# A two-layer trunk whose FFN operands are cut by token halves instead of interleaved tokens

## The chip, the cores and the metric

The program runs on one core of one Trainium2 chip. The metric is the device time of one execution in microseconds (us). Before the change the median of three runs is 2257.63 us (2257.1 to 2259.68).

## The reference

x holds 1024 tokens of 1024 features in float32. Layer 0 mixes tokens by attention, layer 1 by a gated recurrence; each layer then has a SwiGLU FFN of width 2816, and every sub-layer is wrapped in two RMS norms.

```python
def swiglu(h, w_gate, w_up, w_down):
    return (jax.nn.silu(h @ w_gate) * (h @ w_up)) @ w_down

for layer in range(2):
    h = rmsnorm(x, norm_mix_pre[layer])
    m = attention_mixer(h, ...) if layer == 0 else recurrent_mixer(h, ...)   # ends in (...) @ w_out
    x = x + rmsnorm(m, norm_mix_post[layer])
    h = rmsnorm(x, norm_ffn_pre[layer])
    x = x + rmsnorm(swiglu(h, w_gate[layer], w_up[layer], w_down[layer]), norm_ffn_post[layer])
```

## The kernel before

**Stages.** Attention with its input projection; `out_product` (the mixer's output projection, its post-norm, the residual, the FFN's pre-norm); `gate_up`; `down` (with the post-norm, the residual, and the pre-norm of what follows); `recurrent`; then `out_product`, `gate_up` and `down` of layer 1. A token tile is 128 tokens, numbered 0 to 7. A product in almost full precision is made of three passes over fp32r operands: hi times hi, hi times lo, lo times hi, where hi is a cast on ACT and lo the remainder, subtracted on DVE. Every operand therefore costs one ACT and one DVE instruction.

**out_product.** Tiles 0, 1, 2 and then 3, 4, 5 are made in triples, six PSUM buffers each, by three passes; tiles 6 and 7 follow in plain fp32. After each tile `post_norm` runs: multiply by the post gain (DVE, L212), sum of squares (ACT, L164), reciprocal root (POOL, L167 and L168), residual (DVE, L215), store; `pre_norm` then takes a second sum of squares, scales the rows on ACT (L189), transposes them on PE into two PSUM buffers (L197), and hands them to a sink.

**gate_up.** Each 256 columns of a weight times the hidden state is one Strassen product of the Winograd kind: 7 products of 128 x 512 instead of 8, of 4 blocks and 3 passes each, 84 matmuls. There are 11 pairs of columns for gate and 11 for up in a layer. The left operands (A11, A12, S2, S3, S1, S4, A22) are made from the weight tile, which ACT first scales by the FFN's norm weights (L478); the right ones are seven combinations of the hidden state's four blocks B11, B12, B21, B22: features in halves by tokens in halves. `HiddenS` holds them: its group b0 is B11 and B21, b1 is B22, b2 the four sums.

**Which tokens are a half.** Before, the two halves of the tokens are interleaved: in every tile of 128, the first 64 tokens are of one half and the last 64 of the other. So each tile fills 64 columns of all seven operands (L80 to L96), and after four tiles the first 256 of their 512 columns are complete. The first gate pair of a layer uses this: `strassen` runs for `early` (256 columns, from tiles 0 to 3) and again for `late`.

**down.** It uses the same scheme and gives its rows in the same interleaving: `norm(r, a)` holds two runs of 64 tokens, with r the half and a the block. `rows()` loads x and stores the result for each as two DMAs of 64 rows; the last stage's second halves are stored over ACT's queue. The blocks of r = 1 are normed first, while the last products run; then for a = 0 to 3 the last product's eleven steps are followed by `norm(0, a)`. After layer 0, `HiddenT` takes the rows, and a pair (r, a) lies in token half a//2, which `recurrent` reads in halves of 512 tokens, half 0 first (L757 to L764).

**What sets the order.** A scheduler with a timeline model orders the instructions of each engine when the kernel is built; each engine then runs its list in order. Buffers are rings (`bufs=`): a tile waits until the last reader of the one before it in the ring is done. `self.psum()` has six PSUM buffers, `psum_t` (transposes) two. DMAs are issued in order on SP's queue.

Of the kernel before, what the change touches and what calls it, by code (L numbers as in the profile page):

```python
# [8 lines left out]
F32 = mybir.dt.float32  # L9
# [6 lines left out]
P = 128  # L16
# [11 lines left out]
def rows(t, x):  # L28

    if not isinstance(t, tuple):  # L30
        return [(slice(0, P), x[t * P:(t + 1) * P, :])]
    r, a = t
    o = [2 * a * P + k * P + 64 * r for k in range(2)]
    return [(slice(64 * k, 64 * k + 64), x[o[k]:o[k] + 64, :]) for k in range(2)]


class HiddenT:
# [7 lines left out]
    def take(self, t, pst, scratch, pool):  # L45
        nc = self.nc
        if isinstance(t, tuple):
            r, a = t
            hh, hl = (h.rearrange("p k (a t r i) -> p k a t r i", a=2, t=2, r=2)[:, :, a % 2, :, r, :]
                      for h in self.half[a // 2])  # L50
            pst = [ps.rearrange("p a (t i) -> p a t i", t=2) for ps in pst]
        else:
            tok = slice((t % 4) * P, (t % 4) * P + P)
            hh, hl = (h[:, :, tok] for h in self.half[t // 4])
        for q, ps in enumerate(pst):
            hi = hh[:, 4 * q:4 * q + 4]
            self.last = nc.scalar.copy(hi, ps).ins
            nc.vector.tensor_tensor(hl[:, 4 * q:4 * q + 4], ps, hi.bitcast(F32), op=ALU.subtract)


class HiddenS:
# [8 lines left out]
    def __init__(self, trunk, pool):  # L70
        self.nc, self.uid = trunk.nc, trunk.uid
        self.g = [[pool.tile([P, n, 4, 512], F32R, tag=f"b{i}{z}", name=trunk.uid("hS"))
                   for z in range(2)] for i, (_, n) in enumerate(self.GROUPS)]

    def op(self, i, z, kt, cols):
        for (i0, n), g in zip(self.GROUPS, self.g):
            if i0 <= i < i0 + n:
                return g[z][:, i - i0, kt, cols]

    def take(self, t, pst, scratch, pool):  # L80
        nc = self.nc
        hf = scratch.rearrange("p (q a b) -> p q a b", q=2, a=4)
        for q, ps in enumerate(pst):
            nc.scalar.copy(hf[:, q], ps)
        lo, hi = slice(0, 64), slice(64, P)
        b11, b12, b21, b22 = hf[:, 0, :, lo], hf[:, 0, :, hi], hf[:, 1, :, lo], hf[:, 1, :, hi]
        tf = pool.tile([P, 4, 4, 64], F32, tag="tf", bufs=1, name=self.uid("tf"))
        sub = lambda o, x, y: nc.vector.tensor_tensor(o, x, y, op=ALU.subtract)  # L88
        sub(tf[:, 0], b12, b11)
        sub(tf[:, 2], b22, b12)  # L90
        sub(tf[:, 1], b22, tf[:, 0])
        sub(tf[:, 3], tf[:, 1], b21)
        cols = slice(64 * t, 64 * t + 64)
        for src, (h, l) in zip((hf[:, :, :, lo], hf[:, 1:2, :, hi], tf), self.g):
            self.last = nc.scalar.copy(h[:, :, :, cols], src).ins  # L95
            sub(l[:, :, :, cols], src, h[:, :, :, cols].bitcast(F32))  # L96


class Trunk:
# [101 lines left out]
    def post_norm(self, ms, mg, x_src, x_dst, t, gpost, sink, pool):  # L201
# [4 lines left out]
        for d, s in rows(t, x_src):  # L206
            self.load(x[d, :], s)
# [8 lines left out]
        for k, (d, s) in enumerate(rows(t, x_dst)):  # L216
            (nc.scalar if k and sink is None else nc.sync).dma_start(s, x[d, :])
        if sink is not None:
            self.pre_norm(pool, x, mg, None, sink, t, self.psum_t)
# [188 lines left out]
    def out_product(self, ap, aT, w, x_src, x_dst, gpost_v, sink, kts):  # L408
# [4 lines left out]
        def act(kt, t0, n, pool, bufs, tag="act"):  # L413
            a = pool.tile([P, 384], F32, tag=tag, bufs=bufs, name=self.uid("act"))[:, :n * P]
            nc.sync.dma_start(a, aT[kt][:, t0 * P:(t0 + n) * P])
            return a
# [8 lines left out]
        def norm(t, ps):  # L425
            mg = ap.tile([P, D], F32, tag="mg", bufs=3, name=self.uid("mg"))
            ms = [(slice(i * 512, (i + 1) * 512), p) for i, p in enumerate(ps)]
            self.post_norm(ms, mg, x_src, x_dst, t, gpost, sink, ap)

        gpost = None  # L430
        for t0 in (0, 3):
            pst = [[self.psum() for _ in range(2)] for _ in range(3)]
            for kt in kts:
                pool, bufs = (self.apool, 1) if t0 == 0 and kt == kts[0] else (ap, 3)
                a = act(kt, t0, 3, pool, bufs)
                wh, wl = self.split(wv[kt], 2, 512)
                ah, al = (pool.tile([P, 384], F32R, tag=n, bufs=bufs, name=self.uid(n)) for n in ("ah", "al"))
# [6 lines left out]
            if gpost is None:  # L444
                gpost = self.gain(ap, "gpost", gpost_v)
            for t in range(3):
                norm(t0 + t, pst[t])

        rows, acts = [], []
        for i, kt in enumerate(kts):  # L450
# [3 lines left out]
            acts.append(act(kt, 6, 2, ap, 3, ("act", "ah", "al")[i % 3]))  # L454
# [7 lines left out]
    def gate_up(self, ap, hS, wg, wu, gain, gO):  # L462
# [4 lines left out]
        nc = self.nc  # L467

        def load(w, j, tags, after=None):

            a = []
            for k in range(2):
                raw = self.main.tile([P, 4, 256], F32, tag="raw", bufs=3, name=self.uid("raw"))
                src = w[k * 512:(k + 1) * 512, j * 256:(j + 1) * 256].rearrange("(k p) c -> p k c", p=P)
                nc.sync.dma_start(raw, src)
                with self.tc.issue_after(after) if after else nullcontext():
                    for i in range(4):
                        nc.scalar.activation(raw[:, i], raw[:, i], AF.Copy, scale=gain[:, 4 * k + i:4 * k + i + 1])  # L478
                a.append(raw)
            a11, a21 = a[0][:, :, 0:P], a[0][:, :, P:256]  # L480
            a12, a22 = a[1][:, :, 0:P], a[1][:, :, P:256]
            q = {}
            for name, tag in zip(("A11", "A12", "S2", "S3", "S1", "S4", "A22"), tags):
                pool, bufs = (self.main, 8) if tag == "w" else (ap, 6)
                q[name] = pool.tile([P, 2, 4, P], F32R, tag=tag, bufs=bufs, name=self.uid("q"))

            def split(n, src):
                t = q[n]
                self.last = nc.scalar.copy(t[:, 0], src).ins  # L489
                nc.vector.tensor_tensor(t[:, 1], src, t[:, 0].bitcast(F32), op=ALU.subtract)  # L490

            tt = nc.vector.tensor_tensor
            split("A11", a11)
            split("A12", a12)
            split("A22", a22)
            tt(a22, a21, a22, op=ALU.add)
            tt(a21, a11, a21, op=ALU.subtract)
            tt(a11, a22, a11, op=ALU.subtract)  # L498
            split("S2", a11)
            split("S3", a21)  # L500
            split("S1", a22)
            tt(a12, a12, a11, op=ALU.subtract)
            split("S4", a12)
            return q

        def product(ps, a, i, cols):
            for kt in range(4):
                bh, bl = hS.op(i, 0, kt, cols), hS.op(i, 1, kt, cols)
# [5 lines left out]
        tt = nc.vector.tensor_tensor  # L514

        def blocks():
            return [ap.tile([P, 512], F32, tag="c", bufs=11, name=self.uid("c")) for _ in range(4)]

        def strassen(c, q, cols):

            s1, u2, u3, c22 = c

            def new():
                return self.psum()[:, :cols.stop - cols.start]

            nc.scalar.copy(s1, product(new(), q["A11"], 0, cols))
            p2 = product(new(), q["A12"], 1, cols)
            tt(u2, product(new(), q["S2"], 4, cols), s1, op=ALU.add)
            tt(s1, p2, s1, op=ALU.add)
            tt(u3, product(new(), q["S3"], 5, cols), u2, op=ALU.add)  # L530
            p5 = product(new(), q["S1"], 3, cols)
            tt(u2, p5, u2, op=ALU.add)
            tt(c22, p5, u3, op=ALU.add)
            tt(u2, product(new(), q["S4"], 2, cols), u2, op=ALU.add)
            tt(u3, u3, product(new(), q["A22"], 6, cols), op=ALU.subtract)

        full, early, late = slice(0, 512), slice(0, 256), slice(256, 512)
        for j in range(NF // 2):
            qg = load(wg, j, ["w"] * 7, self.last if j == 1 else None)
            if j == 0:  # L540

                first = self.main.tile([P, 4, 256], F32, tag="w", bufs=8, name=self.uid("first"))
                strassen([first[:, i] for i in range(4)], qg, early)
                cg = blocks()
                strassen([o[:, late] for o in cg], qg, late)
                for i, o in enumerate(cg):
                    nc.scalar.activation(o[:, early], first[:, i], AF.Silu)
                    nc.scalar.activation(o[:, late], o[:, late], AF.Silu)
            else:
                cg = blocks()  # L550
                strassen(cg, qg, full)
# [394 lines left out]
```

## Time and profile before

| what | value |
|---|---|
| runs | 2257.63 us median (2257.1 to 2259.68) |
| profiled execution | 2262.01 us, of which the span is 2260.2 us |
| granted TensorE clock, mean | 0.993 of full |
| out_product, layer 0 | 518.5 to 616.2 us |
| gate_up, layer 0 | 616.2 to 1047.9 us |
| down, layer 0 | 1047.9 to 1273.8 us |
| recurrent | 1273.8 to 1501.5 us |
| out_product, gate_up, down of layer 1 | from 1501.5, 1599.2 and 2029.1 us |
| last matmul, end of the span | 2250.3, 2260.2 us |

A stage here begins with the start of its first matmul. A row of the view by windows gives a stretch, its length, and then for PE, PEld (PE's weight loads), DVE, ACT and POOL the busy us with the number of instructions, then the mean granted PE clock, the DMA engines' share and their GB/s. A row of groups names line, engine, operation and tile, the count, the busy us and mean ns of one, and behind the second bar the idle us before them with what ended it. A timeline row is start us, us, engine, line, operation, and in brackets the idle time before and what ended it.

### The profile page before, as it was taken

The page shows a single profiled execution, that of the slowest core. Times are in us where ns is not written, and L with a number is a line of the kernel's source. Part 1 is how long each engine was busy: PE and PEld are TensorE (multiplying, and loading weights), DVE is VectorE, ACT ScalarE, POOL GpSimd, SP SyncE. Part 2 cuts the span into 40 slices and gives each one's busy share as a digit, 9 for nine tenths or more (in the row PEclk, how much of TensorE's full clock was granted, in tenths as well). Part 3 has the DMA queues.
Part 4 walks back from the last instruction along what each step waited for, and adds up shares of the span by engine and source line. Part 5 has one row for each costly group of instructions (what it writes and reads, how often), then busy time and mean ns, then how long its engine had stood idle before and what let it go on. Part 6 is the DMA issues. An engine that isn't in the chain of part 4 may idle for free. (4 is left out here: it accounts for less than half of the span.)

```text
span 2260.2 us, 30583 instructions
## 1 busy us (share of the span) xinstructions
PE 2201.2 (97%) x11136; PEld 1802.0 (80%) x11136; DVE 1551.9 (69%) x2514; ACT 1149.1 (51%) x2132; POOL 168.3 (7%) x370
## 2 busy tenths in 40 slices
PE   7999999999999999999999999999999999999997
PEld 6887888877678888888887777887788888888875
DVE  5676765464677767675866787536777767668665
ACT  4544455464665454532446567527755444424443
POOL 2111212131100000000001100001100000000010
PEclk9999999999999999999999999999999999999998
DMA  4101011124623333334558511358233333327466
GB/s 161 52 20 52 20 48 41 59 97 132 230 83 104 114 115 108 102 118 175 187 148 251 155 56 41 94 175 269 76 125 108 100 115 104 107 98 274 126 205 196
DMA packets 187271, 273.63 MB, mean 121 GB/s; under 512 B 13936, under 2 KB 115312, under 8 KB 187120
## 3 DMA queue, kind: packets, MB, share of 16 engines
q1 hardware_dynamic: 186480, 269.58, 38.0%
q10 hardware_dynamic: 640, 2.10, 0.3%
q8 instruction: 87, 1.43, 0.3%
q14 instruction: 64, 0.52, 0.1%
HBM read 206.09 MB, written 65.54 MB: 120 GB/s over the span
## 5 line engine op out<-in xcount | busy, mean ns | idle before, releaser
L509 PE MATMUL ps<-hS,q 128*128 128x512 f32 (+1 forms) x1288 | 490.9, 382 | 3.1 <-ACT hS L95 3.1
L510 PE MATMUL ps<-hS,q 128*128 128x512 f32 (+1 forms) x1288 | 490.9, 381 | 0.0
L511 PE MATMUL ps<-hS,q 128*128 128x512 f32 (+1 forms) x1288 | 489.9, 381 | 0.0
L490 DVE TENSOR_TENSOR q<-raw,q 128x512 fp32r<-128x512 f32 x308 | 204.7, 686 | 179.2 <-ACT q L489 178.7
L509 PEld LDWEIGHTS ps<-hS,q 128*128 128x128 f32 x1288 | 243.3, 189 | 50.2 <-ACT hS L95 3.9
L510 PEld LDWEIGHTS ps<-hS,q 128*128 128x128 f32 x1288 | 243.9, 189 | 46.7 <-DVE hS L88 0.4
L511 PEld LDWEIGHTS ps<-hS,q 128*128 128x128 f32 x1288 | 244.0, 189 | 45.8
L489 ACT CAST q<-raw 128x512 fp32r<-128x512 f32 x308 | 177.8, 616 | 168.8 <-DVE raw L498 130.4
L590 PE MATMUL ps<-o,o 128*128 128x512 f32 x616 | 240.9, 392 | 0.9 <-DVE o L585 0.8
L591 PE MATMUL ps<-o,o 128*128 128x512 f32 x616 | 238.2, 391 | 0.7 <-DVE o L701 0.7
L589 PE MATMUL ps<-o,o 128*128 128x512 f32 x616 | 221.1, 393 | 9.0 <-ACT o L700 5.5
L584 ACT CAST o<-raw 128x512 fp32r<-128x512 f32 x206 | 123.6, 620 | 193.8 <-PE ps L591 56.0
L478 ACT ACTIVATE raw<-raw,gcol 128x256 f32<-128x256 f32 x352 | 150.2, 498 | 139.0 <-DMA raw<-in_ffn_w_up_dram 71.8
L585 DVE TENSOR_TENSOR o<-raw,o 128x512 fp32r<-128x512 f32 x206 | 137.9, 688 | 66.4 <-ACT o L584 65.6
L589 PEld LDWEIGHTS ps<-o,o 128*128 128x128 f32 x616 | 115.7, 188 | 37.2 <-ACT o L700 7.7
L144 DVE TENSOR_TENSOR wlo<-raw,whi 128x1024 fp32r<-128x1024 f32 x76 | 93.4, 1230 | 66.0 <-ACT whi L143 65.1
L590 PEld LDWEIGHTS ps<-o,o 128*128 128x128 f32 x616 | 116.2, 189 | 26.6 <-DVE o L585 2.9
L591 PEld LDWEIGHTS ps<-o,o 128*128 128x128 f32 x616 | 116.1, 188 | 25.5 <-DVE o L701 1.6
L167 POOL TENSOR_SCALAR rs<-ss 128x1 f32<-128x1 f32 x64 | 31.8, 496 | 1270.2 <-ACT junk L164 1171.0
L143 ACT CAST whi<-raw 128x1024 fp32r<-128x1024 f32 x76 | 79.8, 1052 | 58.5 <-PE ps L155 24.7
L358 ACT COPY pt<-tr 128x512 f32<-128x512 f32 (+1 forms) x128 | 65.5, 527 | 78.5 <-PE tr L354 78.0
L154 PE MATMUL psq<-hT,whi 128*128 128x512 f32 x256 | 101.2, 395 | 1.1 <-DVE v L253 1.1
(185 smaller groups left out, 4237.6 us busy)
## 6 DMA issues: line engine op xcount, KB each, us to landing
raw<-in_ffn_w_down_dram SPq DMA_DIRECT2D x96, 256.0 KB, 4.6
raw<-in_ffn_w_gate_dram SPq DMA_DIRECT2D x44, 512.0 KB, 4.1
raw<-in_ffn_w_up_dram SPq DMA_DIRECT2D x44, 512.0 KB, 4.1
gS<-c SPq DMA_DIRECT2D x88, 256.0 KB, 3.6
raw<-gS SPq DMA_DIRECT2D x88, 256.0 KB, 3.0
gA<-c SPq DMA_DIRECT2D x66, 256.0 KB, 3.4
raw<-in_attn_w_in_dram SPq DMA_DIRECT2D x24, 512.0 KB, 3.9
raw<-in_attn_w_out_dram SPq DMA_DIRECT2D x24, 512.0 KB, 4.3
```

The source lines that it names most:

```text
L154: nc.tensor.matmul(ps, wh[:, kt, cols], hh[:, kt, :], start=kt == 0, stop=False)
L478: nc.scalar.activation(raw[:, i], raw[:, i], AF.Copy, scale=gain[:, 4 * k + i:4 * k + i + 1])
L489: self.last = nc.scalar.copy(t[:, 0], src).ins
L490: nc.vector.tensor_tensor(t[:, 1], src, t[:, 0].bitcast(F32), op=ALU.subtract)
L509: nc.tensor.matmul(ps, a[:, 0, kt, :], bh, start=kt == 0, stop=False)
L510: nc.tensor.matmul(ps, a[:, 0, kt, :], bl, start=False, stop=False)
L511: nc.tensor.matmul(ps, a[:, 1, kt, :], bh, start=False, stop=kt == 3)
L584: nc.scalar.copy(t[:, 0], src)
L585: tt(t[:, 1], src, t[:, 0].bitcast(F32), op=ALU.subtract)
L589: nc.tensor.matmul(ps, a[0], b[:, 0], start=first, stop=False)
L590: nc.tensor.matmul(ps, a[0], b[:, 1], start=False, stop=False)
L591: nc.tensor.matmul(ps, a[1], b[:, 0], start=False, stop=last)
```

## The change

`HiddenS` now cuts the tokens into halves: tiles 0 to 3 are the first half, 4 to 7 the second. After tiles 0 to 3 group b0 (B11 and B21) is complete in all 512 columns, while b1 and b2 get their columns from tiles 4 to 7 alone: tile t (4 or more) combines its own transposes with those of tile t-4, which are kept as `f`. `out_product` makes its tiles in the order (0, 1, 4), (2, 3, 5), 6, 7, and norms the second triple as 2, 5, 3. In `gate_up` the `early`/`late` split is gone. The two products that need only b0 (A11 times B11, A12 times B21) of four column pairs, gate 0, up 0, gate 1 and up 1, stand first; those of gate 0 and up 0 are then added up, those of gate 1 and up 1 stay in four PSUM buffers until their pairs come. For these four pairs the left half of the weights is loaded apart, ahead of the whole tile. The FFN's norm weights are no longer multiplied into the weights on ACT but into the rows on DVE (L191, with `g`, loaded once a layer into the place of the first step's operands). `mg` and `act` have two buffers instead of three. In `down` a norm's rows are 128 tokens in order, tile 4r + a, with one DMA for load and one for store; the last stage stores on SP alone.

```diff
 class HiddenT:
     def take(self, t, pst, scratch, pool):
-        if isinstance(t, tuple):
-            r, a = t
-            hh, hl = (h.rearrange("p k (a t r i) -> p k a t r i", a=2, t=2, r=2)[:, :, a % 2, :, r, :]
-                      for h in self.half[a // 2])
...
+        tok = slice((t % 4) * P, (t % 4) * P + P)
+        hh, hl = (h[:, :, tok] for h in self.half[t // 4])
 class HiddenS:
+    def take(self, t, ps, scratch, pool):
+        cols = slice((t % 4) * P, (t % 4) * P + P)
...
+        def split(h, l, src):
+            cast(h, src)
+            sub(l, src, h.bitcast(F32))
+        b0, b1, b2 = self.g
+        if t < 4:
+            f = self.f[t] = new("f", 2)
+            for q in range(2):
+                split(b0[0][:, q, :, cols], b0[1][:, q, :, cols], ps[q])
+                cast(f[:, q], ps[q])
+            return
+        b12, b22 = ps
+        f, e = self.f[t - 4], new("e", 1)
+        cast(e[:, 1], b12)
+        sub(f[:, 0], b12, f[:, 0])
+        split(b1[0][:, 0, :, cols], b1[1][:, 0, :, cols], b22)
+        sub(e[:, 1], b22, e[:, 1])
+        sub(e[:, 0], b22, f[:, 0])
+        sub(f[:, 1], f[:, 1], e[:, 0])
+        for src, i in ((e, slice(1, 3)), (f, slice(0, 4, 3))):
+            split(b2[0][:, i, :, cols], b2[1][:, i, :, cols], src)
 def post_norm
-        for d, s in rows(t, x_src):
-            self.load(x[d, :], s)
+        self.load(x, x_src[t * P:(t + 1) * P, :])
...
-            self.pre_norm(pool, x, mg, None, sink, t, self.psum_t)
+            self.pre_norm(pool, x, mg, g, sink, t, self.psum_t)
 def out_product
-            mg = ap.tile([P, D], F32, tag="mg", bufs=3, name=self.uid("mg"))
+            mg = ap.tile([P, D], F32, tag="mg", bufs=2, name=self.uid("mg"))
...
-        for t0 in (0, 3):
+        for ts in ((0, 1, 4), (2, 3, 5)):
...
+                g = self.gain(self.apool, "first", g_v)
+            for i in ((0, 1, 2) if ts[0] == 0 else (0, 2, 1)):
+                norm(ts[i], pst[i])
 def gate_up
-                        nc.scalar.activation(raw[:, i], raw[:, i], AF.Copy, scale=gain[:, 4 * k + i:4 * k + i + 1])
...
+        def begin(w, j):
+            r = raw()
+            for k in range(2):
+                nc.sync.dma_start(r[:, k], rows(w, k, j * 256, P))
+            a11, a12 = operand(r[:, 0]), operand(r[:, 1])
+            return product(a11, 0), product(a12, 1)
...
+        begun = {}
+        for i in range(4):
+            w, j = (wg, wu)[i % 2], i // 2
+            begun[i] = begin(w, j)
+            if i < 2:
+                begun[i] = sums(*begun[i])
         for j in range(NF // 2):
-            if j == 0:
-                first = self.main.tile([P, 4, 256], F32, tag="w", bufs=8, name=self.uid("first"))
-                strassen([first[:, i] for i in range(4)], qg, early)
-                cg = blocks()
-                strassen([o[:, late] for o in cg], qg, late)
...
+            cg = blocks(wg, j, begun.get(2 * j))
+            for o in cg:
+                nc.scalar.activation(o, o, AF.Silu)
+            cu = blocks(wu, j, begun.get(2 * j + 1), hS.last if j == 0 else None)
 def down
-                    self.post_norm(ms, mg, x_src, x_dst, (r, a), gpost, sink, ap)
+                    self.post_norm(ms, mg, x_src, x_dst, 4 * r + a, gpost, sink, ap)
```

The order of PE's list at the end of layer 0's `down`, before the change: `ps2071` is the last product's last block, `hT1930` and `hT1931` are hi and lo of token half 0 in `HiddenT`, and L154 and L155 are matmuls of `recurrent`.

```order
L589 MATMUL ps2071_11942<-o2019_11675,o2070_11939 128x512
L590 MATMUL ps2071_11942<-o2019_11675,o2070_11939 128x512
L591 MATMUL ps2071_11942<-o2019_11675,o2070_11939 128x512
L154 MATMUL ps2097_12056<-hT1930_11253,whi2081_12030 128x512
L154 MATMUL ps2100_12090<-hT1930_11253,whi2084_12037 128x512
L154 MATMUL ps2103_12124<-hT1930_11253,whi2087_12044 128x512
L155 MATMUL ps2097_12056<-hT1931_11254,whi2081_12030 128x512
```

The same place after the change: `ps2066` is the last product's last block, `m1722` and `m1723` are the rows of the last two norms (tiles 2 and 3), `hT1925` is hi of token half 0 and `hT1927` hi of half 1.

```order
L605 MATMUL ps2066_11648<-o2014_11387,o2065_11645 128x512
L606 MATMUL ps2066_11648<-o2014_11387,o2065_11645 128x512
L201 MATMUL pst2058_11619<-ident_63,m1722_9722 128x128 x4
L201 MATMUL pst2059_11624<-ident_63,m1722_9722 128x128 x4
L201 MATMUL pst2073_11700<-ident_63,m1723_9723 128x128 x4
L201 MATMUL pst2074_11705<-ident_63,m1723_9723 128x128 x4
L158 MATMUL ps2092_11760<-hT1925_10973,whi2076_11734 128x512
L158 MATMUL ps2095_11794<-hT1925_10973,whi2079_11741 128x512
L158 MATMUL ps2098_11828<-hT1925_10973,whi2082_11748 128x512
L158 MATMUL ps2101_11862<-hT1927_10975,whi2076_11734 128x512
```

The transposes of the last two tiles, which stood some 25 rows and more behind the first matmuls of `recurrent`, now stand ahead of them.

ACT's list where layer 0's `gate_up` begins, after the change: `pst1273` and `pst1274` are the transposes of tile 7, `hS1056` is b1, `hS1058` b2 (hi), `raw1304` and `raw1305` the whole weight tiles of the first gate pair, `q1307` the operand S2, L570 the silu.

```order
L75 COPY e1275_6507<-pst1273_6497 128x512
L75 CAST hS1056_5602<-pst1274_6502 128x4x128
L75 CAST hS1058_5604<-e1275_6507 128x8x128
L75 CAST hS1058_5604<-f1233_6356 128x2x4x128
L522 COPY c1282_6626<-ps1279_6599 128x512
L493 CAST q1306_6746<-raw1305_6744 128x512
L522 COPY c1291_6667<-ps1288_6640 128x512
L570 ACT_TABLE_LOAD
L570 ACTIVATE c1281_6625<-c1281_6625 128x512
L493 CAST q1307_6752<-raw1304_6742 128x512
```

S2's cast, the first operand needed behind the products that stand first, comes after all four pieces of tile 7 and after a table load.

PE's list there: `pst1231` and `pst1232` are tile 3's transposes, `hS1054` and `hS1055` hi and lo of b0, `q1277`, `q1278`, `q1286` and `q1287` the first two left operands of gate 0 and of up 0.

```order
L201 MATMUL pst1231_6346<-ident_63,mg1223_6324 128x128 x4
L201 MATMUL pst1232_6351<-ident_63,mg1223_6324 128x128 x4
L507 MATMUL ps1279_6599<-hS1054_5600,q1277_6593 128x512
L507 MATMUL ps1280_6612<-hS1054_5600,q1278_6596 128x512
L507 MATMUL ps1288_6640<-hS1054_5600,q1286_6634 128x512
L507 MATMUL ps1289_6653<-hS1054_5600,q1287_6637 128x512
L508 MATMUL ps1279_6599<-hS1055_5601,q1277_6593 128x512
```

All four open products of the first two pairs follow tile 3's transposes at once, 512 columns wide, where before there were 256-wide ones from `early`.

201 lines of the change are left out of this document (89 added, 112 removed).

## The prediction

> **What bounds the kernel now.** I read the busy shares first, then a table of windows by stage, then the waits of PE.
>
> ```profile
> PE 2201.2 (97%) x11136; PEld 1802.0 (80%) x11136; DVE 1551.9 (69%) x2514; ACT 1149.1 (51%) x2132; POOL 168.3 (7%) x370
> 616.20:1047.90 431.70, 426.32 (x1958) 356.36 (x1957) 316.29 (x520) 213.92 (x429) 3.51 (x7) 0.99 0.32 102
> 642.00:1047.90 405.90, 405.90 (x1816) 337.12 (x1815) 292.95 (x475) 193.53 (x392) 0.00 (x0) 1.00 0.33 103
> 1047.90:1273.80 225.90, 219.14 (x973) 177.22 (x972) 168.81 (x255) 114.60 (x198) 17.98 (x26) 1.00 0.69 211
> 1273.80:1501.50 227.70, 222.00 (x977) 180.95 (x977) 147.60 (x191) 130.12 (x163) 2.23 (x6) 1.00 0.25 73
> 1599.20:2029.10 429.90, 426.30 (x1958) 356.37 (x1957) 314.28 (x516) 211.99 (x425) 2.49 (x6) 0.99 0.32 101
> PE pst L197 <- ACT mg L189: 4.9, 2, 2.9
> PE ps L509 <- ACT hS L95: 3.1, 3, 1.4
> PE ps L589 <- ACT o L700: 5.5, 3, 3.2
> ```
>
> PE is busy 97% of the span. In gate_up from 642 us on it is busy 405.90 of 405.90 us: nothing that ACT or DVE does there is waited for. What the change can win or lose lies where one stage hands its rows to the next, and in the number of matmuls.
>
> **Entering gate_up.**
>
> ```profile
> 629.90:635.30 5.40, 1.09 (x8) 0.85 (x8) 4.88 (x12) 4.37 (x8) 0.93 (x2) 0.87 0.24 99
> 635.30:642.00 6.70, 6.67 (x34) 6.45 (x35) 5.00 (x8) 3.82 (x8) 0.00 (x0) 0.59 0.00 0
> 1611.20:1616.70 5.50, 2.25 (x11) 1.65 (x9) 4.25 (x11) 3.82 (x6) 0.93 (x2) 0.71 0.17 68
> L511 PE MATMUL ps<-hS,q x569: 389/389/389, 660.1 to 1046.3; 128*128 128x512 f32 x190
> L511 PE MATMUL ps<-hS,q x15: 283/283/365, 624.1 to 629.3; 128*128 128x256 f32 x15
> 1271.29 1.09 PE L197 MATMUL pst<-ident,m 128*128 128x128 f32 x8 [0.32 <-ACT m L189]
> 1272.14 0.48 PE L591 MATMUL ps<-o,o 128*128 128x512 f32 x1
> ```
>
> In the third pass alone, 569 matmuls lie between 660.1 and 1046.3: 386.2 / 568 / 3 = 0.2267 us for one of 512 columns. The fifteen of 256 columns give 5.2 / 14 / 3 = 0.12 us, so two halves cost 0.24 for 0.227: the split itself is dear by only 168 x 0.12 - 84 x 0.2267 = 1.1 us a layer. Before, a layer's matmuls are 1764 x 0.2267 + 168 x 0.12 = 420.1 us; the stage took 431.7 and 429.9. The 11.6 and 9.8 us over them are 2.6 for the transposes of three tiles (a tile's eight take 0.85 to 0.87 until the next matmul starts, as at 1271.29), and the stop at 629.9 with the slower clock after it. At 0.59 of the clock, 6.7 us of work lost (1 - 0.59) x 6.7 = 2.7 us; a stop of some 4 us therefore costs about 2.5 us more than itself.
>
> After the change there are 1848 matmuls of 512 columns, 418.9 us, and the same 2.6 us of transposes. What remains is what PE waits for. Ahead of S2, the first operand that needs tiles 4 to 7, PE's list now holds 8 products of 12 matmuls: 96 x 0.2267 = 21.8 us. Let F be the end of tile 7's fp32 product. With three tiles' transposes, two of them behind F (1.74) and one partly (0.87 for a tile), PE is covered until F + 24.4.
>
> ```profile
> L490 DVE TENSOR_TENSOR q<-raw,q 128x512 fp32r<-128x512 f32 x308 | 204.7, 686 | 179.2 <-ACT q L489 178.7
> L215 DVE SCALAR_TENSOR_TENSOR x<-mg,rs,x 128x1024 f32<-128x1024 f32 x20 | 25.6, 1282 | 31.2 <-POOL rs L168 19.8 <-DMA x<-in_x_dram 6.5 <-DMA x<-xs 5.0
> L88 DVE TENSOR_TENSOR hS<-tf,hS 128x1024 fp32r<-128x1024 f32 x16 | 19.6, 1222 | 5.2 <-ACT hS L95 5.2
> 619.94 1.29 DVE L490 TENSOR_TENSOR q<-raw,q 128x512 fp32r<-128x512 f32 x2
> L489 ACT CAST q<-raw 128x512 fp32r<-128x512 f32 x308 | 177.8, 616 | 168.8 <-DVE raw L498 130.4 <-PE ps L511 34.0 <-DVE c L534 2.1
> L95 ACT CAST hS<-tf 128x1024 fp32r<-128x1024 f32 x16 | 16.7, 1044 | 7.4 <-DVE tf L88 7.4
> L742 ACT ACT_TABLE_LOAD x14 | 18.0, 1283 | 0.2
> L526 ACT COPY c<-ps 128x512 f32<-128x512 f32 x42 | 23.9, 570 | 8.0 <-PE ps L511 8.0
> ```
>
> Now DVE. In its new list 42 instructions stand from tile 5's transposes (F - 3.5) to S2's lo: 32 of 512 columns and 10 of 1024, the norm gain (a scalar_tensor_tensor, priced by L215) and the differences e and f among them. Two of 512 in a row took 1.29, so they follow at 0.60; those of 1024 at about 1.15. That is 32 x 0.60 + 10 x 1.15 = 30.7 us, so S2 is ready at F + 27.2 if DVE never waits. It will wait: ACT's list puts S2's cast behind four pieces of tile 7, of which the last, f's cast (1.04), waits for a DVE result. Between it and S2's cast stand a copy (0.57), another operand's cast (0.62), a second copy, a table load (1.28) and a silu (about 0.6, as the copy), then the cast itself (0.62). The first copy I let run beside DVE's last work. So 1.04 + 0.62 + 0.57 + 1.28 + 0.6 + 0.62 = 4.7 us are ACT's alone, with DVE at a stand, as these wait for one another: F + 31.9. Walking the same lists from their beginning gives 2.35 us more, earlier, at the first open product, whose lo operand DVE makes behind tile 6's norm work. So PE stops for 2.35 and 5.1 us (31.9 - 24.4 - 2.35), loses about 2.5 to the clock, and about 1 more at the change of triples, where `mg` with two buffers lets the third tile's residual wait for the first's transposes (0 to 3). Sum: 418.9 + 2.6 + 2.35 + 5.1 + 2.5 + 1 = 432.5. That is **+0.8 and +2.6 us** in the two layers: 84 narrow matmul pairs are saved and the stop stays. Bounds: no wait at all, 421.5 (-10.2 and -8.4); each wait doubled, about +6 each. I take the walk, since the tile of before, with no more DVE work, was also complete only 25 us after F (the slow stretch ends at 642).
>
> The Trainium skill's page "TensorE: Matmul & The Clock Gate", Part 1, says that the array falls to half clock after an idle window of about 3.4 us and needs about 3.4 us of work to come back. By it a stop would cost about 1.7 us, an estimate. The 0.59 over 6.7 us is about twice that, so the trace disagrees on the length; by the page the sum below would be some 2 to 3 us lower.
>
> **ACT's scaling of the weights** goes: 352 instructions, 150 us. It lies beside the fully busy PE of the stretch above, so it is worth nothing; without that cover it would be worth at most its place at the stage's start, which the walk holds.
>
> **From layer 0's down to recurrent.** This is the large term.
>
> ```profile
> 1273.62 0.39 PE L591 MATMUL ps<-o,o 128*128 128x512 f32 x1
> 1273.84 0.84 PE L154 MATMUL ps<-hT,whi 128*128 128x512 f32 x3
> 1275.79 0.50 PE L155 MATMUL ps<-hT,whi 128*128 128x512 f32 x1 [1.10 <-DVE hT L58]
> 1289.99 1.03 PE L197 MATMUL pst<-ident,m 128*128 128x128 f32 x8
> 1276.78 0.69 DVE L706 TENSOR_TENSOR m<-ps,m 128x512 f32<-128x512 f32 x1
> 1280.18 1.23 DVE L139 TENSOR_TENSOR raw<-raw,gcol 128x1024 f32<-128x1024 f32 x1 [2.12 <-DMA raw<-in_rg_w_in_dram]
> 1281.33 1.22 DVE L212 TENSOR_TENSOR m<-m,g 128x1024 f32<-128x1024 f32 x1
> 1282.63 1.28 DVE L215 SCALAR_TENSOR_TENSOR x<-m,rs,x 128x1024 f32<-128x1024 f32 x1
> 1283.95 1.06 ACT L164 ACTIVATE m<-x 128x1024 f32<-128x1024 f32 x1 [1.36 <-DVE x L215]
> 1285.19 0.19 POOL L167 TENSOR_SCALAR rs<-ss 128x1 f32<-128x1 f32 x1 [5.62 <-ACT m L164]
> 1285.46 0.55 POOL L168 TENSOR_TENSOR rs<-rs,neghalf 128x1 f32<-128x1 f32 x1
> 1286.05 1.15 ACT L189 ACTIVATE m<-x,rs 128x1024 f32<-128x1024 f32 x1 [0.47 <-POOL rs L168]
> 1290.63 0.59 ACT L57 CAST hT<-pst 128x512 fp32r<-128x512 f32 x1 [3.43 <-PE pst L197]
> ```
>
> Before, the first matmul of recurrent starts 0.22 us behind the last of down: token half 0 comes from blocks 0 and 1, which were normed long ago, and the chain of the last tile (add, gain, residual, square, POOL, scale) runs from 1276.78 to 1287.2 beside those matmuls. After, the blocks of r = 0 are tiles 0 to 3, so half 0 is complete only with the very last tile, and recurrent still begins with half 0. PE's list puts the transposes of tiles 2 and 3 in front, and nothing behind them can pass, since PE takes its list in order. The same chain then decides: scale done at 1287.2; plus 1.2 for two hT pieces of tile 2 that DVE's list now has ahead of the residual; transposes 1.03; cast 0.59. PE resumes near 1290.0 where before it did at 1273.84: 16.2 us. Off that: 1.7 for the two tiles' transposes, which before lay among the later matmuls, and 1.3 for before's own stop (1273.84 + 3 x 0.227 to 1275.79). On that: 2.4 for the clock after such a stop. **+15.5 us.** Bounds: the 2.12 us for the weight's DMA and the 1.2 vanish and the clock costs 1.7, +11.5; the weight lands 4 us later, +19.5. Queued behind the waiting transposes is all of recurrent; ACT and DVE wait for PE there in turn, and nothing later gives it back, since that stage is PE's (222.0 of 227.7).
>
> **Down's DMAs.**
>
> ```profile
> x<-xs SPq DMA_DIRECT2D x32, 256.0 KB, 5.6
> x<-xs SPq DMA_DIRECT2D x8, 512.0 KB, 4.9
> ```
>
> Half as many loads and stores stand in SP's queue, ahead of the `act` loads behind the 5.5 us at L589. One load of 512 KB lands in 4.9 where a half took 5.6. I take **-1 us** for both downs; bounds -6 (all of L589's waits) and +2. At the very end one store of 512 KB takes the place of two halves on two queues: 0, within 1.
>
> **Sum.** 0.8 + 2.6 + 15.5 - 1 = +17.9 on the profiled 2262.0 us (span 2260.2 and 1.8 around it). That execution is 4.4 above the median of the runs; the difference carries over: 2257.6 + 17.9 = 2275.5, **2275 us**.
>
> **Rivals.** (1) *DVE keeps up*: in both layers S2 is ready when the open products end, the stops and the slow clock vanish (-18.6), and the recurrent term is at its low bound (+11.5): with -1, 2249.5, faster. For it: 21.8 us of cover is new. Against it: 30.7 us of DVE work does not fit into 3.5 + 24.4. It decides from S2 ready by F + 24.4. Chance 0.09. (2) *One layer keeps up*, or both by half, with the low recurrent term: -9 + 11.5 - 1, about 2259, no change. Chance 0.12. (3) *The open products choke the start*: they hold four of six PSUM buffers until the pairs of j = 1, so two buffers serve products whose results DVE must clear while it is late; each product beyond the second waits for one. At about 6 us a layer more, 2287. For it, the list and DVE's load there; against it, 84 matmuls (19 us) need only some eight DVE clears (5 us). Chance 0.14. The forecast keeps 0.65.
>
> A measurement of this kernel tells 0.2% (4.5 us) from no change. Faster 0.09, same 0.12, slower 0.79. The range, 2261 to 2287, leaves out rival 1, half of rival 2 and the upper part of rival 3.
>
> **What would show it.** In the changed profile PE should stand idle about 13 us behind down's last matmul in layer 0, broken only by transposes of tiles 2 and 3 and ended by a cast of hT; the granted clock should be near 0.6 for some 6 us after it; each gate_up should take 430 to 434 us, with a wait of some 5 us for q or hS before the ninth product. I would be wrong if that wait is missing, or if recurrent begins with half 1.

## The result and the profile after

The changed kernel takes 2271.1 us (median of 4, 2269.42 to 2272.06) where the kernel before, on the same chip, takes 2258.65 us: the ratio is 1.0052, with a 95% interval of 1.0035 to 1.0070. It is slower, by 8 to 16 us, inside the range given and on the side that was forecast (2275). The two profiled spans, 2269.7 and 2260.2 us, differ by 9.5 us. The sum was near; two of its terms were far off, and their errors largely cancelled.

The first row of the page of the changed kernel, and its windows, cut at the first matmul of each stage. Three short rows show what lies behind the last matmul of a stage: of out_product in layer 0, of down in layer 0, and of the whole program.

```profile
PE 2201.2 (97%) x10968; PEld 1794.1 (79%) x10968; DVE 1592.3 (70%) x2476; ACT 999.9 (44%) x1738; POOL 163.8 (7%) x370
514.80:616.80 102.00, 98.73 (x393) 71.43 (x392) 58.73 (x71) 48.05 (x90) 11.77 (x30) 0.98 0.67 215
616.80:618.60 1.80, 1.43 (x10) 0.89 (x8) 1.80 (x4) 1.33 (x5) 0.93 (x3) 1.00 0.52 185
618.60:1051.60 433.00, 426.30 (x1868) 350.65 (x1867) 331.21 (x505) 146.46 (x243) 2.41 (x7) 0.99 0.33 103
1051.60:1271.30 219.70, 217.05 (x973) 177.52 (x971) 169.03 (x255) 114.67 (x198) 17.62 (x26) 1.00 0.67 218
1271.30:1287.20 15.90, 4.20 (x18) 3.05 (x17) 9.13 (x12) 7.52 (x12) 2.21 (x6) 0.60 0.49 154
1287.20:1513.70 226.50, 222.04 (x962) 180.90 (x962) 139.54 (x180) 123.24 (x152) 0.00 (x0) 0.99 0.21 66
1513.70:1616.30 102.60, 98.72 (x401) 70.99 (x399) 63.36 (x80) 52.02 (x97) 12.69 (x33) 1.00 0.73 241
1616.30:2048.60 432.30, 424.14 (x1867) 349.84 (x1866) 330.51 (x505) 146.46 (x243) 2.41 (x7) 0.99 0.33 103
2048.60:2261.00 212.40, 210.56 (x925) 172.94 (x924) 156.79 (x242) 94.97 (x172) 12.05 (x17) 1.00 0.64 214
2261.00:2269.70 8.70, 0.08 (x1) 0.00 (x0) 3.71 (x5) 0.72 (x2) 0.93 (x3) 0.68 0.29 121
```

Against the windows of before, from first matmul to first matmul, the 9.5 us between the spans are made up of:

| stretch | before | after | difference |
|---|---|---|---|
| attention | 518.5 | 514.8 | -3.7 |
| out_product, layer 0 and 1 | 97.8, 97.6 | 103.8, 102.6 | +6.0, +5.0 |
| gate_up, layer 0 and 1 | 431.7, 429.9 | 433.0, 432.3 | +1.3, +2.4 |
| down, layer 0, up to recurrent | 225.9 | 235.6 | +9.7 |
| recurrent | 227.7 | 226.5 | -1.2 |
| down, layer 1, to the end of the span | 231.1 | 221.1 | -10.0 |

The waits of PE that matter in the changed kernel (total us, times, longest), and PE and ACT around the end of down in layer 0:

```profile
PE pst L201 <- ACT m L193: 12.3, 4, 8.4
PE ps L507 <- ACT c L522: 10.1, 3, 5.3
PE ps L432 <- ACT junk L168: 6.5, 2, 3.3
1271.07 0.39 PE L606 MATMUL ps<-o,o 128*128 128x512 f32 x1
1274.73 2.20 PE L201 MATMUL pst<-ident,m 128*128 128x128 f32 x8 [3.27 <-ACT m L193]
1285.36 1.97 PE L201 MATMUL pst<-ident,m 128*128 128x128 f32 x8 [8.43 <-ACT m L193]
1287.15 2.07 PE L158 MATMUL ps<-hT,whi 128*128 128x512 f32 x4
1284.16 1.15 ACT L193 ACTIVATE m<-x,rs 128x1024 f32<-128x1024 f32 x1 [0.94 <-POOL rs L172]
1286.51 0.58 ACT L42 CAST hT<-pst 128x512 fp32r<-128x512 f32 x1 [1.21 <-PE pst L201]
```

From the last matmul of down (1271.07) to the first of recurrent (1287.15) pass 16.08 us, with the transposes of tiles 2 and 3 inside and the cast of hT at the end; the prediction said 16.2 and named these pieces. The other two waits are new: one in the out product, where L432 waits for the square sums of the tile before (L168), and one in gate_up, where a product waits for ACT's copy at L522.

### The profile page after: what moved, and what is told of

It is laid out like the page before. It is cut to its first block, busy times and chain, and to the rows that moved or that the text cites. A ratio compares the mean times of both kernels' runs of the same rounds, so it can differ in the third digit from the quotient of the medians.

```text
span 2269.7 us, 29965 instructions
## 1 busy us (share of the span) xinstructions
PE 2201.2 (97%) x10968; PEld 1794.1 (79%) x10968; DVE 1592.3 (70%) x2476; ACT 999.9 (44%) x1738; POOL 163.8 (7%) x370
## 5 line engine op out<-in xcount | busy, mean ns | idle before, releaser
L507 PE MATMUL ps<-hS,q 128*128 128x512 f32 x1232 | 482.6, 392 | 13.4 <-ACT c L522 10.1
L508 PE MATMUL ps<-hS,q 128*128 128x512 f32 x1232 | 481.7, 391 | 1.5 <-DVE hS L78 1.5
L509 PE MATMUL ps<-hS,q 128*128 128x512 f32 x1232 | 481.0, 391 | 0.0
L493 ACT CAST q<-raw 128x512 fp32r<-128x512 f32 x308 | 187.0, 621 | 410.5 <-PE ps L509 154.4
L507 PEld LDWEIGHTS ps<-hS,q 128*128 128x128 f32 x1232 | 232.4, 189 | 65.0 <-ACT c L522 11.2
L508 PEld LDWEIGHTS ps<-hS,q 128*128 128x128 f32 x1232 | 232.7, 189 | 50.4 <-DVE hS L78 2.3
L509 PEld LDWEIGHTS ps<-hS,q 128*128 128x128 f32 x1232 | 232.5, 189 | 48.6
L171 POOL TENSOR_SCALAR rs<-ss 128x1 f32<-128x1 f32 x64 | 25.7, 401 | 1267.4 <-ACT junk L168 1174.4
L158 PE MATMUL psq<-hT,whi 128*128 128x512 f32 x256 | 101.2, 395 | 1.1 <-DVE v L255 1.1
L159 PE MATMUL psq<-hT,whi 128*128 128x512 f32 x256 | 100.9, 394 | 0.0
L160 PE MATMUL psq<-hT,wlo 128*128 128x512 f32 x256 | 100.5, 393 | 0.0
```

Source lines behind the costliest of these rows:

```text
L158: nc.tensor.matmul(ps, wh[:, kt, cols], hh[:, kt, :], start=kt == 0, stop=False)
L159: nc.tensor.matmul(ps, wh[:, kt, cols], hl[:, kt, :], start=False, stop=False)
L507: nc.tensor.matmul(ps, a[:, 0, kt, :], bh, start=kt == 0, stop=False)
L508: nc.tensor.matmul(ps, a[:, 0, kt, :], bl, start=False, stop=False)
L509: nc.tensor.matmul(ps, a[:, 1, kt, :], bh, start=False, stop=kt == 3)
```

## The experiments

Each edit is to the changed kernel. Every kernel was timed beside its own runs of the kernel before, whose medians lie between 2257.7 and 2260.4 us. The changed kernel stands 12.5 us above its own, and "against the changed kernel" below is how much more or less than 12.5 us another one stands above its own. As these medians alone differ by up to 2.7 us, differences of that size tell little.

### The halves exchanged

```diff
 def take(self, t, ps, scratch, pool):
+        t = (t + 4) % 8
 def out_product
-        for ts in ((0, 1, 4), (2, 3, 5)):
+        for ts in ((4, 5, 0), (6, 7, 1)):
...
-            norm(6 + t, ps)
+            norm(2 + t, ps)
 def down
-                    self.post_norm(ms, mg, x_src, x_dst, 4 * r + a, gpost, sink, ap)
+                    self.post_norm(ms, mg, x_src, x_dst, 4 * (1 - r) + a, gpost, sink, ap)
```

> The changed kernel with the two token halves exchanged: tiles 4 to 7 take the place of 0 to 3 in the operands, the out product makes (4, 5, 0), (6, 7, 1), 2, 3, and down's early norms give tiles 0 to 3, its late ones 4 to 7. So token half 0 is complete long before down ends. My theory (recurrent waits for half 0, which only the last tile completes): the 15.9 us between the last matmul of down and the first of recurrent in layer 0 fall below 2 us, and the stage behind is about as long, so the time is 13 to 15 us below the changed kernel's: 2256 to 2258. Rival (the stop comes from the weights of recurrent or from the chain of the norm itself, whichever half it is): the stop stays above 10 us and the time within 3 us of 2271.

Measured: 2256.53 us, 14.4 below the changed kernel; 0.9991 of before (0.9981 to 1.0000). PE at the same place, and the only wait that is left there between 1250 and 1300 us:

```profile
1271.27 0.48 PE L606 MATMUL ps<-o,o 128*128 128x512 f32 x1
1271.58 0.40 PE L607 MATMUL ps<-o,o 128*128 128x512 f32 x1
1271.82 0.39 PE L160 MATMUL ps<-hT,whi 128*128 128x512 f32 x1
PE ps L159 <- ACT hT L42: 0.2, 1, 0.2
```

Recurrent follows down at the matmuls' own distance; some of its matmuls even stand among down's last ones. The weights and the norm's chain are the same as in the changed kernel, so neither made the stop: it was the half that is asked for first and finished last. The rival falls.

### Three mg buffers

```diff
-            mg = ap.tile([P, D], F32, tag="mg", bufs=2, name=self.uid("mg"))
+            mg = ap.tile([P, D], F32, tag="mg", bufs=3, name=self.uid("mg"))
...
-        f, e = self.f[t - 4], new("e", 1)
+        f, e = self.f[t - 4], scratch.rearrange("p (q a b) -> p q a b", q=2, a=4)
```

> The changed kernel with three mg buffers instead of two; the room comes from keeping e in the mg tile that the transposes have read instead of in a tile of its own. My theory (the third tile's post-norm waits for the first's transposes to free its mg, and PE for that post-norm to free PSUM): the stop of 3.3 us on L168 in both out products and the slower clock behind it vanish, 4 to 5 us each, so 2261 to 2264. Rival (the stop comes from the longer chain through DVE, since the norm weights now go on the rows there): the stop stays above 2 us in each, and the time within 3 us of 2271.

Measured: 2265.28 us, 5.7 below the changed kernel. The first window goes from out_product's first matmul to its last, the second from there to gate_up's first:

```profile
515.00:613.00 98.00, 96.89 (x386) 69.45 (x385) 58.45 (x70) 47.79 (x90) 14.89 (x35) 1.00 0.69 224
613.00:617.10 4.10, 2.02 (x15) 1.26 (x13) 4.10 (x8) 2.28 (x4) 0.00 (x0) 1.00 0.74 217
PE ps L432 <- ACT junk L168: 2.2, 4, 0.6
```

Out_product's own matmuls take 98.0 us instead of 102.0 (in layer 1, 97.7 instead of 100.8), as before the change: the stop of 3.3 us and the slower clock behind it (0.98 against 1.00 in layer 0) were the ring's. In layer 0 PE idles 1.1 us instead of 3.3, so of the 4.0 us 2.2 are waiting and the rest the clock; short waits at L432 remain, 0.6 us at the longest. But 2.3 of the 4.0 us come back at once, since 4.1 us instead of 1.8 lie ahead of gate_up: PE now arrives earlier at the last transposes, and waits 1.4 us there for DVE (`f`, L78). So the mechanism is as expected and the gain a little over half of what was expected.

### Whole DMAs or halves

The changed kernel's loads of x, its stores, or both, in `down`, as two DMAs of 64 rows; and the loads as two of 128 rows by 512 columns.

```diff
-        self.load(x, x_src[t * P:(t + 1) * P, :])
+        for d in (slice(0, 64), slice(64, P)):
+            self.load(x[d, :], x_src[t * P + d.start:t * P + d.stop, :])
...
-        nc.sync.dma_start(x_dst[t * P:(t + 1) * P, :], x)
+        for d in (slice(0, 64), slice(64, P)):
+            nc.sync.dma_start(x_dst[t * P + d.start:t * P + d.stop, :], x[d, :])
```

> The changed kernel with down's loads of x and stores of the result as two DMAs of 64 rows each, as before the change, the rows in token order as after it. My theory (down became 6 us shorter in layer 0, 9 in layer 1 and 1 at the very end because half as many DMAs stand ahead of the act loads): down grows again by 10 to 16 us in all, 2281 to 2287. Rival (the shorter down comes from the other order of the lists, or from the contiguous rows themselves): down stays within 3 us of the changed kernel's, 2269 to 2274.

> The changed kernel with down's loads of x alone as two DMAs of 64 rows, its stores whole. The run with both split was 16.5 us above the changed kernel. If it is the loads, which stand ahead of the act loads on SP's queue and which the norm waits for: 10 to 17 us above it, 2281 to 2288. If it is the stores: within 3 us of 2271. If each counts by its DMAs: 2276 to 2281.

> The changed kernel with down's stores alone as two DMAs of 64 rows on SP's queue, its loads whole. If the loads carry the whole difference between the changed kernel and the run with both split: within 3 us of 2271. If each DMA more on SP's queue costs alike, as much as for the loads: 2281 to 2287.

And the columns:

```diff
+        for d in (slice(0, 512), slice(512, D)):
+            self.load(x[:, d], x_src[t * P:(t + 1) * P, d])
```

> The changed kernel with each of down's loads of x as two DMAs of 128 rows by 512 columns instead of one of 128 by 1024. The run with the loads as two of 64 rows was 14 us above the changed kernel. If the number of DMAs on SP's queue is the cause (in that run SP waited 11.5 us at these loads for earlier act loads and 9.9 for stores, which it does not in the changed kernel): the same 10 to 16 us, 2281 to 2287. If it is that 64 rows reach half of the partitions only: within 4 us of 2271.

| kernel | us | above its before | against the changed kernel |
|---|---|---|---|
| loads and stores as 64 rows | 2287.61 | 29.1 | +16.7 |
| loads as 64 rows | 2285.21 | 26.0 | +13.5 |
| stores as 64 rows | 2278.33 | 18.0 | +5.5 |
| loads as 512 columns | 2272.24 | 11.9 | -0.6 |

Down of layer 1, from its first matmul to its last, in the kernel before, then with the loads as 64 rows, then as 512 columns:

```profile
2029.10:2250.30 221.20, 214.15 (x925) 174.02 (x923) 157.15 (x242) 95.04 (x172) 11.88 (x17) 0.98 0.66 206
2057.90:2279.40 221.50, 215.12 (x923) 174.39 (x921) 156.57 (x242) 95.21 (x172) 12.05 (x17) 0.98 0.67 206
2053.30:2264.20 210.90, 209.40 (x921) 172.23 (x919) 157.34 (x242) 94.72 (x172) 11.87 (x17) 1.00 0.65 217
```

The changed kernel's own row for this stretch is 212.40. With 64 rows down is back at what it was before the change (221.20); with as many DMAs that reach all 128 partitions it is not. So it is not their number, as I had priced it. Of the causes that were named, the one left is that each reaches half of the partitions. The runs do not show how that costs time, and the lists are not quite the same: in down of layer 1 PE's is, but those of SP, ACT and DVE differ in a few places. The waits on SP's queue that the last expectation quotes (11.5 us for act loads, 9.9 for stores) are no sign of the number either: the changed kernel has them too, 8.6 and 7.3 us. The loads carry most of the loss, the stores 5.5 us, which neither case of their expectation had; together they cost less than the two apart. The median landing of a load says little (5.4 us for 64 rows, 4.9 for 512 columns). The loss shows as 6.4 us in which PE idles (221.50 - 215.12) against 1.8 in the changed kernel, and as a clock of 0.98 against 1.00. With both split, 14.7 of the 16.7 us lie in down (4.5 in layer 0, 10.1 in layer 1, 0.1 behind the last matmul), of the 16.2 that it had become shorter by.

### The norm weights on the weights again

```diff
+                for i in range(4):
+                    nc.scalar.activation(r[:, i], r[:, i], AF.Copy, scale=gain[:, 4 * k + i:4 * k + i + 1])
...
-            self.pre_norm(pool, x, mg, g, sink, t, self.psum_t)
+            self.pre_norm(pool, x, mg, None, sink, t, self.psum_t)
```

> The changed kernel with the FFN's norm weights on the weight tiles again (ACT), the rows scaled on ACT without them. My theory (DVE's 1.28 us a tile for the norm weights lies in the chain into gate_up, while ACT's 150 us lie beside a busy PE): out product and gate_up together change by less than 4 us a layer, with the sign open: 2264 to 2278. Rival (freeing ACT is what keeps the first pairs short): ACT's eight scalings for each of the first weight tiles, about 4 us a tile, delay the open products and gate_up grows by 4 to 8 us a layer: 2279 to 2287.

Measured: 2304.7 us, 33.7 above the changed kernel, which neither theory had. In layer 0 out_product is 3.3 and gate_up 11.7 us longer, in layer 1 7.9 and 12.0. Each kernel from early in gate_up of layer 0 to 720 us, first this one, then the changed one; and this one's longest waits:

```profile
624.00:720.00 96.00, 82.69 (x336) 65.68 (x337) 62.80 (x95) 52.90 (x101) 3.65 (x10) 0.91 0.25 83
618.60:720.00 101.40, 94.70 (x405) 76.07 (x404) 86.83 (x133) 42.11 (x71) 2.41 (x7) 0.95 0.33 107
PE ps L507 <- ACT c L524: 14.4, 2, 8.2
PE ps L507 <- DVE c L558: 5.6, 7, 1.2
```

PE idles 13.3 us of the first stretch, 6.7 of the second. The longest wait for ACT's copy that frees a PSUM buffer is 8.2 us instead of 4.6 and 5.3, and the scalings stand in ACT's list too. The run also moves the scaling of the rows back from DVE to ACT, so it does not tell the two apart. That ACT's 150 us lie beside a busy PE was true of the middle of gate_up before the change. It says nothing of the stage's first 100 us once four pairs are opened there.

### The open products' buffers and the first silu

In the changed kernel PE has done only six of the eight open products (72 matmuls) when it stops ahead of the seventh:

```profile
640.50 0.40 PE L509 MATMUL ps<-hS,q 128*128 128x512 f32 x1
645.54 0.80 PE L507 MATMUL ps<-hS,q 128*128 128x512 f32 x1 [4.64 <-ACT c L522]
643.96 1.04 ACT L75 CAST hS<-f 128x1024 fp32r<-128x1024 f32 x1
644.91 0.58 ACT L522 COPY c<-ps 128x512 f32<-128x512 f32 x1
```

All six PSUM buffers are held until ACT copies the first product out, behind tile 7's casts. That looked like the cause of the stop, against the prediction's (the chain of operands on DVE and ACT).

```diff
-            begun[i] = begin(w, j)
+            begun[i] = begin(w, j, self.psum_t if i == 3 else self.psum)
```

> The changed kernel with the two open products of up 1 in the two PSUM buffers of the transposes instead of in the general six. Theory from the changed kernel's trace (72 matmuls run, and the stop of about 5 us stands ahead of the seventh open product: it waits for a PSUM buffer, which ACT's copy of the first product frees only behind tile 7's casts): the seventh and eighth run without a stop, and one of 2 to 4 us is left ahead of the ninth, whose operand S2 ACT casts behind a table load and a silu. Each gate_up becomes 2 to 4 us shorter, 2262 to 2267 in all. Rival (my prediction's mechanism, the stop is DVE's and ACT's chain of operands, the buffers have no part in it): each gate_up stays within 1 us.

Measured: 2270.25 us, 1.4 below the changed kernel, and gate_up 432.5 and 432.2 us instead of 433.0 and 432.3. The stop has moved behind the eighth product and is about as long as it was (the first two rows; below them the end of the silu on ACT, the sum for S2 on DVE at L544, what DVE does next, and S2's cast):

```profile
645.68 0.39 PE L509 MATMUL pst<-hS,q 128*128 128x512 f32 x1
651.24 0.79 PE L507 MATMUL ps<-hS,q 128*128 128x512 f32 x1 [5.17 <-DVE raw L548]
647.52 0.63 ACT L570 ACTIVATE c<-c 128x512 f32<-128x512 f32 x1
649.80 0.69 DVE L544 TENSOR_TENSOR raw<-raw,raw 128x512 f32<-128x512 f32 x1
650.52 0.69 DVE L548 TENSOR_TENSOR raw<-raw,raw 128x512 f32<-128x512 f32 x1
650.57 2.18 ACT L493 CAST q<-raw 128x512 fp32r<-128x512 f32 x4 [2.42 <-issue]
```

So the new theory fell. The buffers set where PE stops; when it can go on is set by DVE, which after tile 7's work still has the sums of the first pairs and of S2 to make, and by ACT, which casts S2 at 650.57, as soon as DVE's sum is there. That S2 comes late by a chain through DVE and ACT is what the prediction had. But the last engine in it is DVE, not ACT's own list as in its walk: ACT is done with the silu at 648.15 and idles 2.42 us. The view names no releaser for this, but the cast starts 0.08 us behind the end of DVE's sum (650.49).

```diff
-            for o in cg:
-                nc.scalar.activation(o, o, AF.Silu)
+            with self.tc.issue_after(self.last) if j == 0 else nullcontext():
+                for o in cg:
+                    nc.scalar.activation(o, o, AF.Silu)
```

> The kernel with up 1's open products in the transposes' buffers, and besides the first pair's silu ordered behind the casts of its operands. Theory: S2's cast comes 1.9 us earlier (1.28 for the table load, 0.63 for the silu), and what is left of the stop ahead of the ninth product shrinks by 1 to 2 us in each layer against the run without this. Rival (the ninth product then waits for DVE's lo of b2 and of S2): less than 0.7 us a layer.

Measured: 2271.97 us, 0.3 above the changed kernel, no difference; gate_up is 432.1 and 431.4, 0.5 and 0.9 less than without. ACT reaches S2's cast earlier and idles the longer for it:

```profile
652.49 2.18 ACT L493 CAST q<-raw 128x512 fp32r<-128x512 f32 x4 [3.89 <-issue]
```

The table load and the silu were not what S2 waited for.

### The terms together

> The changed kernel with the token halves exchanged and three mg buffers (e kept in mg), without the two edits on the open products and the silu. If the two terms add up (-14.6 and -5.8 against 2271.1): 2250 to 2252, and the other two edits were worth 2 to 4 us in the run with all four (2247.9). If those two edits were worth nothing, as alone: within 1.5 us of 2247.9.

Measured: 2251.25 us, 0.9967 of before (0.9958 to 0.9976), 18.9 below the changed kernel where the two terms alone gave 14.4 + 5.7 = 20.1.

> The changed kernel with four of the edits together: the token halves exchanged, three mg buffers (e kept in mg), up 1's open products in the transposes' buffers, the first silu behind the operands. If the terms add up (-14.6 for the halves, -5.8 for mg, -4 to -8 for the buffers, -2 to -4 for the silu, all against the changed kernel's 2271.1): 2239 to 2247, below both kernels. If the edits at the entry of gate_up only move one wait onto the next, as part of the mg edit did: 2247 to 2252.

Measured: 2247.91 us, 0.9951 of before (0.9939 to 0.9964), 23.8 below the changed kernel and the fastest of all. The terms did not all add up, as the second case had it. By the stages the two small edits are worth 0.4 and 1.3 us in gate_up here (430.0 and 430.4 to 429.6 and 429.2); the medians put them at 3.3 to 4.9 us, which is hardly more than the baselines differ by.

## Why the prediction was right, and where not

**The stop ahead of recurrent: right.** 16.08 us against 16.2, ended by the pieces that were named. With the longer path taken off and the clock's loss put on, 15.5 were expected; the exchange of halves gave 14.4 back. The weight's DMA (2.12) came out as 1.6. The clock's loss can be counted in the changed kernel's row at 1287.15 and those behind it:

```profile
1289.02 0.63 PE L159 MATMUL ps<-hT,whi 128*128 128x512 f32 x1
1289.45 0.63 PE L160 MATMUL ps<-hT,wlo 128*128 128x512 f32 x1
1289.88 0.63 PE L158 MATMUL ps<-hT,whi 128*128 128x512 f32 x1
1290.30 0.63 PE L159 MATMUL ps<-hT,whi 128*128 128x512 f32 x1
1290.73 0.63 PE L160 MATMUL ps<-hT,wlo 128*128 128x512 f32 x1
1291.16 0.52 PE L158 MATMUL ps<-hT,whi 128*128 128x512 f32 x1
```

Nine matmuls from 1287.15 to 1291.16 took 4.0 us where 9 x 0.2267 = 2.0 are usual. So this stop cost 2.0 us more than itself, not the 2.4 of the sum. The estimate of 1.7 us by the Trainium skill's page "TensorE: Matmul & The Clock Gate", Part 1, was somewhat nearer. The 2.4 came from gate_up before the change. There the slow stretch is as long as in gate_up of the changed kernel, but more work lay in it (before, then after):

```profile
633.90:640.70 6.80, 5.37 (x24) 5.15 (x24) 4.86 (x11) 3.89 (x7) 0.00 (x0) 0.50 0.00 1
642.90:649.70 6.80, 4.16 (x10) 3.29 (x11) 6.38 (x10) 5.39 (x7) 0.00 (x0) 0.50 0.00 0
```

At half the clock that is a loss of about 2.7 and 2.1 us. What a stop cost beyond itself hung on how much of the slow stretch fell on work.

**Gate_up itself: right in time, with one step of its walk wrong.** Without the 1 us put there for mg, 431.5 was expected (-0.2 and +1.6 against 431.7 and 429.9), and 433.0 and 432.3 measured (+1.3 and +2.4): the waits took back what the wide matmuls saved. The wait of about 5 us is there in both layers (4.6 and 5.3), the one at the first open product too (0.9 and 0.7 for the 2.35 expected); rivals 1 and 2, in which DVE keeps up, did not come about. The long wait stands ahead of the seventh product, not the ninth as "what would show it" had it, because the prediction took PSUM to hold all eight; rival 3 named the buffers, but not that they stop PE before DVE does. The buffer experiment shows that this changed the place and hardly the time. The step that failed is the end of the walk, 4.7 us in which ACT was to work alone "with DVE at a stand". In the trace DVE has no pause over 0.4 us there, and ACT is the one that idles. DVE's pauses lie earlier, in the norm of tile 6 and its transposes, and the 30.7 us for its 42 instructions had none:

```profile
630.27 1.28 DVE L195 SCALAR_TENSOR_TENSOR mg<-x,rs,g 128x1024 f32<-128x1024 f32 x1 [2.13 <-POOL rs L172]
633.38 0.69 DVE L78 TENSOR_TENSOR f<-pst,f 128x512 f32<-128x512 f32 x1 [1.82 <-ACT e L75]
```

With the shorter ones behind them they come to 5.8 us. S2's cast ends at 651.5, 34.1 us behind the end of tile 7's product (617.4), where the walk had 31.9. So 4.7 us in the wrong place stood for 5.8 in the right one, and that the stop was met this closely is partly luck.

**The step on mg: mis-sized.** "About 1 more at the change of triples (0 to 3)" measured 4.0 and 3.1 us, as the run with three buffers shows, with a stop of 3.3 us in each layer; and out_product is +6.0 and +5.0 in all. The other 2 us lie between its last product and gate_up's first (1.8 us), where tile 3 has to be complete before the first wide product, which the 256-wide ones of before did not need.

**Down's DMAs: wrong in size and in mechanism.** "-1 us for both downs", with -6 as the bound, measured about -6.2 in layer 0 (225.7 to 219.5 from first to last matmul), -8.7 in layer 1 (220.8 to 212.0) and -1.3 in the tail. I bounded it by the 5.5 us that PE was seen to wait at L589, and priced the DMAs by their number. But the windows of before showed 6.8 and 7.0 us of idle PE in the two stages (225.90 - 219.14, 221.20 - 214.15), more than that one wait. The two rows for a load that the prediction quotes (256 KB in 5.6 us, 512 KB in 4.9) could not have told it: the eight of 512 KB belong to out_product, and in the changed kernel, where down's loads are whole, the median of all 24 is 5.3. The Trainium skill's page "SBUF — State Buffer", section "Door 1: The DMA port swizzle", has the rule that should have been weighed: a transfer on partitions 0 to 63 or 64 to 127 reaches only 8 of the 16 ports. Its section "Can I just issue two DMAs to hit both halves?" adds that two such transfers do not make up for it. The runs agree in what they cost: two loads of 64 rows +13.5 us, two of 128 rows -0.6. They do not show the ports.

**ACT's scaling "worth nothing": wrong outside its cover.** The cover was named (PE busy 405.90 of 405.90 us), but that stretch is the middle of the stage. At its start, in the new order, it is not covered: with it put back (and the rows' scaling back on ACT), out_product and gate_up together are 15.0 and 19.9 us longer.

**Attention was taken as unchanged.** It became 3.7 us shorter. 1.8 of it is chance: PE's list is the same up to 480 us, and from 36 us on the two traces run 1.78 us apart, because the clock was granted at another moment:

```profile
20.00:40.00 20.00, 16.04 (x109) 15.84 (x110) 14.47 (x19) 6.54 (x11) 7.49 (x12) 0.83 0.44 123
20.00:40.00 20.00, 16.24 (x124) 16.03 (x125) 14.83 (x20) 8.12 (x14) 7.26 (x12) 0.91 0.45 126
```

(Before, then after.) All the kernels made from the changed one begin out_product at 514.5 to 517.2 us, in two groups about 1.8 apart. The other 1.9 us belong to the order: near the end of attention, where the loads of out_product's first operands changed, the scheduler's list is another one, and before's waits of 2.3 us for `pso` at L363 shrink to 0.4.

Taken together: +14.7 instead of +3.4 in entering gate_up with the out product; 14.7 instead of 15.5 for the stop (16.1, less 0.2 for a matmul's distance and the 1.2 that recurrent got shorter); -16.2 instead of -1 in down; -3.7 instead of 0. The errors of the first and the third, +11.3 and -15.2, largely cancel. The right total is partly luck.

## What to carry to other kernels

Where work in one order feeds work in another, ask which piece the reader wants first and whether it is the one that the writer finishes last; here renaming the halves was worth 14.4 us at no cost. Load and store rows over all 128 partitions: splitting the loads by columns cost nothing that could be measured, and splitting them by partitions 13.5 us. Work on an engine that is free on the average over a stage need not be free at the stage's start.

## What was not expected of the hardware

Two loads of 64 rows and two of 512 columns move the same bytes by as many transfers, and the one kernel is 14 us slower (2285.21 to 2272.24, 26.0 and 11.9 above their own runs of before). Why is not shown by these runs. Between two profiled executions, the moment at which the full clock was granted in the first 35 us moved everything behind it, up to 470 us, by 1.78 us.
